# A one-core hybrid decoder block: TensorE's work put in written order, gates moved ahead of branch products, PSUM banks dealt out anew

## The chip, the cores and the metric

The kernel runs on one core of a Trainium2 chip. The metric is the device time of one execution in microseconds (us), lower is better. Three runs of the kernel before took 1508.08 us in the median (1503.97 to 1508.12). The profiled execution is a run of its own.

## What is computed

One decoder layer on 256 tokens of width 2048, in float32. The reference, cut to what matters:

```python
h = rmsnorm(x, norm_g)
proj = einsum('bsd,df->bsf', h, w_in)            # 2048 -> 18432 columns, 14 parts
ya = stick_breaking_attention(a_q, a_k, a_v) * silu(a_g)            # 8 heads of 128
yb = silu(layernorm(causal_depthwise_conv(b_a * sigmoid(b_b)))) * silu(b_g)   # width 31
yc = gelu(c_u) * spatial_mix(layernorm(gelu(c_v))) * silu(c_g)
yd = dilated_mixture(d_q, d_k, d_v) * silu(d_g)                     # 8 heads, 3 patterns
yproj = einsum('bsnc,ncd->bsnd', stack([ya, yb, yc, yd]), w_branch) # 4 x (1024 -> 2048)
gates = sigmoid(einsum('bsd,df->bsf', h, w_gate) + b_gate)          # 2048 -> 4 x 2048
x = x + einsum('bsd,de->bse', sum(gates * yproj), w_out)
out = rmsnorm(x, final_g)
```

## The kernel before

**Weights.** All weights stand in one array of blocks of 128x2048 floats, in the order in which they are used (`weight_plan`, L35). A block is fetched by one 1 MB DMA into one of three `st` buffers (L117). To keep float32 accuracy at the speed of a reduced format, each half block is split in two: ScalarE copies it rounded into `hi` (L130) and VectorE subtracts that from the original into `lo` (L131). There are five `hi` and five `lo` buffers of 128x1024; a half block's buffers come free when TensorE has used them, so up to two and a half blocks are ready ahead. The splits are put 300 instructions ahead in priority (L140).

**Two forms of product.** In the *feature form* (`mm_t`, L238) a block gives 128 features for all 256 tokens: 16 steps over the 2048 inputs, each a product of 512 columns (L245: hi weights by the activations' hi and lo parts side by side) and one of 256 columns (L248: lo weights by the hi part). `proj_t` (L272) makes two such features tiles in the two banks of one PSUM tile of `ps_mm`; `evac` (L264) then adds the two column halves, by ScalarE (L266) and VectorE (L267), for both features at once. A *pair* below is such a pair of blocks. In the *token form* (`mm_n`, L278) a block is the moving operand: 24 products of 512 columns (L286 to L288), for both halves of the tokens. Four blocks make 512 output columns over all 2048 inputs, two over a branch's 1024.

**Order of the stages.** d_v in the token form (with unnormalised x, while `make_h`, L213, computes the norm and writes the normalised activations' parts to `xhl`); b_a and b_b with their product `glu`; the 8 heads of d, each three pairs of q and k with their `scores`, `softmax`, `transpose` and `values` (L420 to L473); the layer norm of the convolution (L493); the gate stage of d; b_g and the gate stage of b; a_v, four head pairs of a (L532), the gate stage of a; c_v, the eight tiles of c, its gate stage; the output projection with the final norm.

**A gate stage** (`gate_proj`, L358) has four column blocks of 512. For each one: two bias products (L369) and 96 products into a `ps_mm` tile of two banks, ScalarE's sigmoid into `gt` (L375), then 48 products of the branch into the `ps_2` tile `psy`, which VectorE multiplies with the gate (L382, L384) and adds to `merged` (L385). In the last stage `sink` (L637) then transposes that block of `merged` (L642) and splits it into `mh` and `ml` for the output projection.

**What sets the order.** The program is written in one order; a scheduler that plays it through with estimated times then fixes each engine's instruction order: of the instructions whose inputs it expects to be ready it takes the one written first, priorities considered. That holds for all engines, TensorE too. The small products of the attention heads are written between the large ones by `later(n, fn)` and `tick` (L147 to L159): `fn` is written when n more ticks have passed. A pair has one tick, a gate block three. `flush` (L161) ends all that is pending at once; it stands ahead of each gate stage and behind the last. The 31 taps of the convolution for 8 channel blocks (L402 to L412, 248 VectorE instructions, mostly L412) are written nine at a time between the pairs of d, with a priority 100 lower; they only need `glu`, so they can be taken whenever VectorE has nothing older.

**PSUM** has 8 banks of 512 floats per partition: `ps_mm` two tiles of two banks (feature pairs, token blocks, gates, output, transposes of `sink`), `ps_2` one tile of two banks (branch products, attention's transposes and sums), `ps_s` two tiles of one bank (scores).

**The sums of an a pair** (L553): four products for the first of two heads into the first bank of `cc` (L557 to L560), VectorE's subtraction of it from `zm` (L561), then the same for the second head in the second bank.

Of the kernel before, what the change touches and what calls it, by code (L numbers as in the profile page):

```python
# [31 lines left out]
BRANCH = dict(a=0, b=1, c=2, d=3)  # L32


def weight_plan():  # L35

    plan = []

    def t(name, i):
        plan.append(("in", OFF[name] // P + i))  # L40

    def n(name):
        for c in range(2):
            for q in range(4):
                plan.append(("inN", OFF[name] // 512 + c, q))

    def gate(b):
        for c in range(4):
            for q in range(4):
                plan.append(("gateN", BRANCH[b] * 4 + c, q))  # L50
            for q in range(2):
                plan.append(("brN", BRANCH[b], c, q))
# [42 lines left out]
def hybrid_block(ctx: ExitStack, tc, w, x, xT, vec, bg, cst, dmask, sgu_wT, sgu_lg, sgu_lb, sgu_b, final_g, out):  # L95
# [117 lines left out]
    def make_h():  # L213
# [11 lines left out]
        T.matmul(pst[:, :S], ones, red[:, 0, :], start=True, stop=False)  # L225
        T.matmul(pst[:, :S], ones, red[:, 1, :], start=False, stop=True)
        rsqrt(rstd[:], pst[:, :S], float(D), [P, S])
        for q in range(4):
            for k in range(4 * q, 4 * q + 4):
                V.scalar_tensor_tensor(xt[:, k, :], xt[:, k, :], norm_g(k), rstd[:], op0=ALU.mult, op1=ALU.mult)  # L230
            ks = slice(4 * q, 4 * q + 4)
            split(xhl[:, ks, 0:S], xhl[:, ks, S:2 * S], xt[:, ks, :])
        for b in range(2):
# [4 lines left out]
    def mm_t(ps, j, weights, rhs, nk):  # L238

        for k in range(nk):  # L240
            hi, lo = weights[k // 8]
            o = (k % 8) * P

            def full(start, stop):
                T.matmul(ps[:, j, :], hi[:, o:o + P], rhs[:, k, :], start=start, stop=stop)  # L245

            def half():
                T.matmul(ps[:, j, 0:S], lo[:, o:o + P], rhs[:, k, 0:S], start=False, stop=False)  # L248

            if k < nk - 1:  # L250
# [6 lines left out]
    def unit_t(e0, e1):  # L257
        ps = ps_mm.tile([P, 2, 512], F32, tag="mm", name="ps")
        mm_t(ps, 0, next_weights(e0), xhl, KD)
        mm_t(ps, 1, next_weights(e1), xhl, KD)  # L260
        tick()
        return ps

    def evac(ps, dst):  # L264
        bt = ev_p.tile([P, 2, S], F32, tag="bt", name="bt")
        A.activation(bt[:], ps[:, :, S:2 * S], AF.Copy)  # L266
        V.tensor_add(dst, ps[:, :, 0:S], bt[:])  # L267
# [29 lines left out]
    def first_weights(q, expect):  # L297
# [17 lines left out]
        return res  # L315

    def proj_n(name, c, step=None, first=False):
        ps = ps_mm.tile([P, 2, 512], F32, tag="mm", name="psn")
        for q in range(4):
# [5 lines left out]
            if step is not None:  # L325
                step()
        if first and c == 0:
            make_h()
        return ps

    def proj_v(name, step=None, first=False):
        v = t8_p.tile([P, 2, BW], F32, tag="t8", name="v")
        for c in range(2):
            ps = proj_n(name, c, step=step, first=first)
            for tb in range(2):
# [21 lines left out]

    def gate_proj(b, y, first=False, sink=None, step=None):  # L358

# [4 lines left out]

        for c in range(4):
            g = bi * 4 + c
# [7 lines left out]
            gt = gt_p.tile([P, 2, 512], F32, tag="gt", name="gt")  # L374
            A.activation(gt[:], ps[:], AF.Sigmoid)  # L375
# [4 lines left out]
            m = merged[:, :, c * 512:(c + 1) * 512]  # L380
            if first:
                V.tensor_mul(m, psy[:], gt[:])  # L382
            else:
                V.tensor_mul(gt[:], psy[:], gt[:])  # L384
                V.tensor_add(m, m, gt[:])  # L385
            if sink is not None:
                later(1, lambda c=c: sink(c))
            if step is not None:
                step()

# [83 lines left out]

    for h0 in range(0, NH, 2):
        sg = proj_t(ft("d_g", h0), ft("d_g", h0 + 1))
        A.activation(sg[:], sg[:], AF.Silu)
        conv(9)
        d_head(h0, sg)
        d_head(h0 + 1, sg)  # L480


    def chan_sum(src):
        red = ev_p.tile([P, 2, S], F32, tag="bt", name="red")
        V.tensor_reduce(red[:, 0, :], src.rearrange("p c t -> p t c"), axis=AX.X, op=ALU.add)
        ps = ps_2.tile([P, 2, 512], F32, tag="a2", name="pcs")
        T.matmul(ps[:, 0, 0:S], ones, red[:, 0, :], start=True, stop=True)
        return ps[:, 0, :]

    def bc8(ap):  # L490
        return ap.unsqueeze(1).to_broadcast([P, KB, S])

    def conv_norm():  # L493
        pm = chan_sum(cv[:])
        mean = sm_p.tile([P, S], F32, tag="mean", bufs=1, name="mean")
# [3 lines left out]
        A.activation(csq[:], cv[:], AF.Square)  # L499
        pv = chan_sum(csq[:])  # L500
        rsqrt(mean[:], pv[:, 0:S], float(BW), [P, S])
        V.tensor_mul(cv[:], cv[:], bc8(mean[:]))
# [4 lines left out]
    conv_norm()  # L507
    flush()
    gate_bias()
# [6 lines left out]
    for i in range(0, 8, 2):  # L516
        bg = proj_t(ft("b_g", i), ft("b_g", i + 1))
        A.activation(bg[:], bg[:], AF.Silu)
        V.tensor_mul(bg[:], bg[:], cv[:, i:i + 2, :])
        put_y(yb, i, 2, bg[:])  # L520

    flush()
    gate_proj("b", yb)


# [6 lines left out]
    def a_pair(h0):  # L532
        sg = proj_t(ft("a_g", h0), ft("a_g", h0 + 1))
        A.activation(sg[:], sg[:], AF.Silu)
        zm = sc_p.tile([P, 2, 384], F32, tag="e1", bufs=1, name="zm")
# [45 lines left out]

    flush()
    gate_proj("a", ya)


# [39 lines left out]
    for i in range(8):  # L625
        ug = proj_t(ft("c_u", i), ft("c_g", i))
        A.activation(ug[:, 0, :], ug[:, 0, :], AF.Gelu_apprx_tanh)
        A.activation(ug[:, 1, :], ug[:, 1, :], AF.Silu)
        later(2, lambda i=i, ug=ug: c_mix(i, ug))

    flush()

# [4 lines left out]
    def sink(c):  # L637
        pt = ps_mm.tile([P, 4, S], F32, tag="mm", name="pt")
        for f in range(4):
            for tb in range(2):  # L640
                o = c * 512 + f * P
                T.transpose(pt[:, f, tb * P:(tb + 1) * P], merged[:, tb, o:o + P], ident)  # L642
        ks = slice(4 * (c % 2), 4 * (c % 2) + 4)
        A.activation(mh[c // 2][:, ks, :], pt[:], AF.Copy)
        V.tensor_sub(ml[c // 2][:, ks, :], pt[:], mh[c // 2][:, ks, :].bitcast(F32))

    gate_proj("c", yc, sink=sink)
    flush()

# [47 lines left out]
    for tb in range(2):  # L697
        ps = ps_mm.tile([P, 2, 512], F32, tag="mm", name="pso")
        for q in range(4):
# [65 lines left out]
```

## Time and profile before

| what | us |
|---|---|
| median of three runs | 1508.08 |
| the profiled execution's own time | 1508.27 |
| its span in the profile | 1506.6 |
| TensorE busy (98%) | 1479.1 |
| VectorE busy (63%) | 944.4 |
| ScalarE busy (50%) | 760.2 |
| weights read by DMA at 185 GB/s over the span | 277.18 MB |

PE is TensorE's products, PEld its weight loads, DVE is VectorE, ACT is ScalarE, SP and POOL issue DMAs. Products are pipelined: a product of 512 columns is shown as 0.39 us long but the next begins 0.23 us after it, so a busy TensorE is read from the starts and from the idle time in brackets, not from the lengths. "DVE lo L131" is the instruction of line 131 that writes the tile `lo`. The views used below are the page's overview, the list of waits, the table of time windows, the timeline of one engine in a window, and the answer for one source line.

### The profile page before, as it was taken

The page shows a single profiled execution, that of the slowest core. Times are in us where ns is not written, and L with a number is a line of the kernel's source. Part 1 is how long each engine was busy: PE and PEld are TensorE (multiplying, and loading weights), DVE is VectorE, ACT ScalarE, POOL GpSimd, SP SyncE. Part 2 cuts the span into 40 slices and gives each one's busy share as a digit, 9 for nine tenths or more (in the row PEclk, how much of TensorE's full clock was granted, in tenths as well). Part 3 has the DMA queues.
Part 4 walks back from the last instruction along what each step waited for, and adds up shares of the span by engine and source line. Part 5 has one row for each costly group of instructions (what it writes and reads, how often), then busy time and mean ns, then how long its engine had stood idle before and what let it go on. Part 6 is the DMA issues. An engine that isn't in the chain of part 4 may idle for free.

```text
span 1506.6 us, 18648 instructions
## 1 busy us (share of the span) xinstructions
PE 1479.1 (98%) x7484; PEld 1255.4 (83%) x7484; DVE 944.4 (63%) x1249; ACT 760.2 (50%) x860; POOL 10.2 (1%) x22
## 2 busy tenths in 40 slices
PE   7999999999999999999999999999999999999997
PEld 5888888888888788888888888887888888888786
DVE  8899999866566754555545455554545666555454
ACT  7644445564454644454444466654444667444352
POOL 0000000000000000000000000000000000000000
PEclk9999999999999999999999999999999999999999
DMA  8555554445444555555555545444555555555562
GB/s 302 211 195 184 180 187 177 169 166 191 173 168 170 201 203 186 192 195 189 186 186 195 194 168 172 168 177 154 196 195 195 181 183 198 200 190 177 192 217 84
DMA packets 41318, 280.47 MB, mean 186 GB/s; under 512 B 4784, under 2 KB 4784, under 8 KB 8592
## 3 DMA queue, kind: packets, MB, share of 16 engines
q1 hardware_dynamic: 38880, 272.00, 50.5%
q0 software_dynamic: 1632, 6.24, 1.3%
q8 instruction: 58, 0.95, 0.3%
q10 hardware_dynamic: 720, 1.06, 0.2%
q14 instruction: 28, 0.23, 0.0%
HBM read 277.18 MB, written 2.10 MB: 185 GB/s over the span
## 4 chain that ended last, share of the span: by engine, by line
PE 97%; ACT 1%; DVE 1%; DMA 1%; issue 0%; DVEq 0%; ACTq 0%
PE ps L245 30%; PE ps L248 15%; PE psg L286 8%; PE psg L288 8%; PE psg L287 8%; PE psy L286 4%; PE psy L288 4%; PE psy L287 4%; PE psn L287 3%; PE psn L288 3%; PE psn L286 3%; PE pso L286 2%; PE pso L287 2%; PE pso L288 2%; DMA xt<-in_xT_dram 0%; PE psg L369 0%
## 5 line engine op out<-in xcount | busy, mean ns | idle before, releaser
L131 DVE TENSOR_TENSOR lo<-st,hi 128x1024 fp32r<-128x1024 f32 (+1 forms) x506 | 616.0, 1219 | 460.7 <-ACT hi L130 459.2
L130 ACT ACTIVATE hi<-st 128x1024 fp32r<-128x1024 f32 (+1 forms) x506 | 533.4, 1056 | 671.7 <-PE ps L245 262.3
L245 PE MATMUL ps<-xhl,hi 128*128 128x512 f32 x1920 | 675.5, 398 | 0.0
L248 PE MATMUL ps<-xhl,lo 128*128 128x256 f32 x1920 | 519.5, 281 | 0.0
L245 PEld LDWEIGHTS ps<-xhl,hi 128*128 128x128 f32 x1920 | 355.2, 188 | 74.6
L248 PEld LDWEIGHTS ps<-xhl,lo 128*128 128x128 f32 x1920 | 362.3, 189 | 9.6
L286 PE MATMUL psg<-hi,xhl 128*128 128x512 f32 x512 | 201.0, 393 | 1.1 <-ACT hi L130 1.1
L288 PE MATMUL psg<-hi,xhl 128*128 128x512 f32 x512 | 200.3, 391 | 0.0
L287 PE MATMUL psg<-lo,xhl 128*128 128x512 f32 x512 | 200.2, 391 | 0.0
L286 PEld LDWEIGHTS psg<-hi,xhl 128*128 128x128 f32 x512 | 96.4, 188 | 21.6 <-ACT hi L130 1.7
L288 PEld LDWEIGHTS psg<-hi,xhl 128*128 128x128 f32 x512 | 96.6, 189 | 20.2
L287 PEld LDWEIGHTS psg<-lo,xhl 128*128 128x128 f32 x512 | 96.6, 189 | 20.0
L412 DVE SCALAR_TENSOR_TENSOR cv<-glu,vec_sb,cv 128x255 f32<-128x255 f32 (+26 forms) x240 | 100.8, 463 | 0.2
L286 PE MATMUL psy<-hi,y 128*128 128x512 f32 x256 | 99.6, 389 | 0.0
L287 PE MATMUL psy<-lo,y 128*128 128x512 f32 x256 | 99.6, 389 | 0.0
L288 PE MATMUL psy<-hi,y 128*128 128x512 f32 x256 | 99.6, 389 | 0.0
L288 PEld LDWEIGHTS psy<-hi,y 128*128 128x128 f32 x256 | 48.1, 188 | 10.0
L287 PEld LDWEIGHTS psy<-lo,y 128*128 128x128 f32 x256 | 48.1, 188 | 10.0
L286 PEld LDWEIGHTS psy<-hi,y 128*128 128x128 f32 x256 | 48.1, 188 | 9.9
L286 PE MATMUL psn<-hi,xhl 128*128 128x512 f32 x128 | 49.8, 389 | 0.0
L287 PE MATMUL psn<-lo,xhl 128*128 128x512 f32 x128 | 49.8, 389 | 0.0
L288 PE MATMUL psn<-hi,xhl 128*128 128x512 f32 x128 | 49.8, 389 | 0.0
(207 smaller groups left out, 1105.2 us busy)
## 6 DMA issues: line engine op xcount, KB each, us to landing
st<-in_w_dram SPq DMA_DIRECT2D x254, 1024.0 KB, 4.8
xr<-in_x_dram POOLq DMA_DIRECT2D x8, 256.0 KB, 3.9
xt<-in_xT_dram SPq DMA_DIRECT2D x3, 512.0 KB, 8.7
st<-in_w_dram SPq DMA_DIRECT2D x4, 256.0 KB, 5.3
st<-in_w_dram SPq DMA_DIRECT2D x2, 512.0 KB, 7.4
fg<-in_final_g_dram POOLq DMA_DIRECT2D x1, 1024.0 KB, 6.8
out_dram<-r SPq DMA_DIRECT2D x4, 256.0 KB, 3.2
out_dram<-r ACTq DMA_DIRECT2D x4, 256.0 KB, 3.5
```

The costliest lines, as they stand in the source:

```text
L130: A.activation(hi, src, AF.Copy)
L131: V.tensor_sub(lo, src, hi.bitcast(F32))
L245: T.matmul(ps[:, j, :], hi[:, o:o + P], rhs[:, k, :], start=start, stop=stop)
L248: T.matmul(ps[:, j, 0:S], lo[:, o:o + P], rhs[:, k, 0:S], start=False, stop=False)
L286: T.matmul(ps[:, tb, :], lh(k0 + kk, 0, tb), hi[:, o:o + 512], start=st, stop=False)
L287: T.matmul(ps[:, tb, :], lh(k0 + kk, 0, tb), lo[:, o:o + 512], start=False, stop=False)
L288: T.matmul(ps[:, tb, :], lh(k0 + kk, 1, tb), hi[:, o:o + 512], start=False, stop=sp)
L412: V.scalar_tensor_tensor(dst, src, wc, dst, op0=ALU.mult, op1=ALU.add)
```

## The change

- **TensorE in written order.** `tc.manual_schedule(engines={PE})`: TensorE's instructions run in the order in which the program writes them; the other engines are still ordered by the scheduler.
- **Gate stage.** The four gate blocks g0 to g3, branch products y0 to y3 and sinks s0 to s2 are written as g0 g1 y0 g2 s0 y1 g3 s1 y2 y3 s2; the plan of weights follows. Sink 3 stands in the output projection's first block, ahead of its last quarter.
- **PSUM.** `ps_mm` has one tile of two banks; two tiles of one bank (`ps_t`) take the feature tiles, each evacuated by itself, and `sink`'s transposes in two halves. The token blocks and output blocks alternate between `ps_mm` and `ps_2`. `make_h`'s and the channel sums' products move to `ps_s`.
- **`make_h`** is written in three pieces: its squares and sums behind d_v's first block, its sum products and what follows behind the first quarter of the second block, the products for `rstd_n` behind the third quarter. d_v's blocks are both evacuated after both are written.
- **The convolution's norm** is written in three pieces from d's head 6 on, one and three pairs ahead of the gate stage; the remaining taps are written there.
- **The flushes are gone**: what is pending at the end of a stage is written at the ticks of the gate stage that follows.

The diff, cut to its core:

```diff
+GATE_ORDER = [(e[0], int(e[1])) for e in "g0 g1 y0 g2 s0 y1 g3 s1 y2 y3 s2".split()]
...
-    ps_mm = ctx.enter_context(tc.tile_pool(name="psm", bufs=2, space=bass.MemoryType.PSUM))
+    ps_t = ctx.enter_context(tc.tile_pool(name="pst", bufs=2, space=bass.MemoryType.PSUM))
+    ps_mm = ctx.enter_context(tc.tile_pool(name="psm", bufs=1, space=bass.MemoryType.PSUM))
     ps_2 = ctx.enter_context(tc.tile_pool(name="ps2", bufs=1, space=bass.MemoryType.PSUM))
     ps_s = ctx.enter_context(tc.tile_pool(name="pss", bufs=2, space=bass.MemoryType.PSUM))
+
+    ctx.enter_context(tc.manual_schedule(engines={mybir.EngineType.PE}))
...
         V.tensor_add(red[:], red[:], rd2[:])
-        pp = ps_2.tile([P, 2, 512], F32, tag="a2", name="pp")
-        pst, psn = pp[:, 0, :], pp[:, 1, :]
+        yield
+        pst = ps_s.tile([P, 512], F32, tag="s", name="pst")
         T.matmul(pst[:, :S], ones, red[:, 0, :], start=True, stop=False)
...
-    def proj_t(e0, e1):
-        ps = unit_t(e0, e1)
+    def proj_t(e0, e1, funcs=(None, None)):
+
         dst = qk_p.tile([P, 2, S], F32, tag="qk", name="dst")
-        evac(ps, dst[:])
+        for j, e in enumerate((e0, e1)):
+            ps = ps_t.tile([P, 512], F32, tag="t", name="ps")
+            mm_t(ps, next_weights(e), xhl)
+            bt = ev_p.tile([P, S], F32, tag="bt", name="bt")
+            A.activation(bt[:], ps[:, S:2 * S], AF.Copy)
+            V.tensor_add(dst[:, j, :], ps[:, 0:S], bt[:])
+            if funcs[j] is not None:
+                A.activation(dst[:, j, :], dst[:, j, :], funcs[j])
+        tick()
         return dst
...
     def proj_n(name, c, step=None, first=False):
-        ps = ps_mm.tile([P, 2, 512], F32, tag="mm", name="psn")
+        ps = (ps_2.tile([P, 2, 512], F32, tag="a2", name="psn") if c else
+              ps_mm.tile([P, 2, 512], F32, tag="mm", name="psn"))
...
+            if first and c and q in (0, 2):
+                next(parts[0])
         if first and c == 0:
-            make_h()
+            parts.append(make_h())
+            next(parts[0])
...
+        gts = {}
+
+        def gate(c):
             g = bi * 4 + c
             ps = ps_mm.tile([P, 2, 512], F32, tag="mm", name="psg")
...
+            gts[c] = gt_p.tile([P, 2, 512], F32, tag="gt", name="gt")
+            A.activation(gts[c][:], ps[:], AF.Sigmoid)
+
+        def branch(c):
             psy = ps_2.tile([P, 2, 512], F32, tag="a2", name="psy")
             for q in range(2):
                 mm_n(psy, next_weights(("brN", bi, c, q)), 4 * q, y_lh, q == 0, q == 1)
             tick()
...
+        for s, c in GATE_ORDER:
+            if s != "s":
+                (gate if s == "g" else branch)(c)
+            elif sink is not None:
+                sink(c)
...
+        if h0 == 6:
+            conv(len(taps))
+            conv_norm()
+        d_head(h0 + 1, sg)
...
-    flush()
     gate_proj("a", ya)
...
     def sink(c):
-        pt = ps_mm.tile([P, 4, S], F32, tag="mm", name="pt")
-        for f in range(4):
...
+        for f0 in (0, 2):
+            pt = ps_t.tile([P, 2, S], F32, tag="t", name="pt")
+            for f in range(2):
...
     for c in range(3):
-        ps = ps_mm.tile([P, 2, 512], F32, tag="mm", name="pso")
+        ps = (ps_2 if c % 2 else ps_mm).tile([P, 2, 512], F32, tag="a2" if c % 2 else "mm", name="pso")
         for q in range(4):
+            if c == 0 and q == 3:
+                sink(3)
             mm_n(ps, next_weights(("out", c, q)), 4 * q, m_lh, q == 0, q == 3)
```

More of the change, by code (lines that the diff above doesn't have):

```diff
@@ L47, in gate @@
     def gate(b):
[L48 to L52, printed above, removed]
+        for s, c in GATE_ORDER:
+            if s == "g":
+                for q in range(4):
+                    plan.append(("gateN", BRANCH[b] * 4 + c, q))
+            elif s == "y":
+                for q in range(2):
+                    plan.append(("brN", BRANCH[b], c, q))
     n("d_v")
@@ L232, in make_h @@
             split(xhl[:, ks, 0:S], xhl[:, ks, S:2 * S], xt[:, ks, :])
+        yield
+        psn = ps_s.tile([P, 512], F32, tag="s", name="psn")
         for b in range(2):
@@ L235, in make_h, with mm_t @@
         V.tensor_copy(rstd_n[:], psn[:, 0:2])
-    def mm_t(ps, j, weights, rhs, nk):
-        for k in range(nk):
+        yield
+    def mm_t(ps, weights, rhs):
+        for k in range(KD):
             hi, lo = weights[k // 8]
@@ L332, in proj_v @@
         v = t8_p.tile([P, 2, BW], F32, tag="t8", name="v")
-        for c in range(2):
-            ps = proj_n(name, c, step=step, first=first)
+        pss = [proj_n(name, c, step=step, first=first) for c in range(2)]
+        for c, ps in enumerate(pss):
             for tb in range(2):
@@ L356, in gate_bias, with gate_proj @@
         V.tensor_sub(bgr[32:64, :], b[32:64, :], bgr[32:64, :].bitcast(F32))
-    def gate_proj(b, y, first=False, sink=None, step=None):
+    def gate_proj(b, y, first=False, sink=None):
         bi = BRANCH[b]
@@ L363, in y_lh @@
             return y[:, k, part * S + tb * P:part * S + (tb + 1) * P]
-        for c in range(4):
+        gts = {}
+        def gate(c):
             g = bi * 4 + c
@@ L379, in gate_proj @@
             tick()
-            m = merged[:, :, c * 512:(c + 1) * 512]
+            m, gt = merged[:, :, c * 512:(c + 1) * 512], gts.pop(c)
             if first:
@@ L385, in gate_proj @@
                 V.tensor_add(m, m, gt[:])
[L386 to L389, printed above, removed]
+        for s, c in GATE_ORDER:
+            if s != "s":
+                (gate if s == "g" else branch)(c)
+            elif sink is not None:
+                sink(c)
     vd = proj_v("d_v", first=True)
@@ L473, in d_head, with chan_red, chan_sum, conv_norm2 @@
             later(1, lambda g=g, qk=qk, qs=qs: scores(g, qk, qs))
[L475 to L488, printed above, removed]
     def bc8(ap):
         return ap.unsqueeze(1).to_broadcast([P, KB, S])
+    def chan_red(src):
+        red = ev_p.tile([P, S], F32, tag="bt", name="red")
+        V.tensor_reduce(red[:], src.rearrange("p c t -> p t c"), axis=AX.X, op=ALU.add)
+        return red
+    def chan_sum(red):
+        ps = ps_s.tile([P, 512], F32, tag="s", name="pcs")
+        T.matmul(ps[:, 0:S], ones, red[:], start=True, stop=True)
+        return ps
     def conv_norm():
-        pm = chan_sum(cv[:])
+        red = chan_red(cv[:])
+        later(1, lambda: conv_norm2(red))
+    def conv_norm2(red):
+        pm = chan_sum(red)
         mean = sm_p.tile([P, S], F32, tag="mean", bufs=1, name="mean")
@@ L499, in conv_norm, with conv_norm3 @@
         A.activation(csq[:], cv[:], AF.Square)
-        pv = chan_sum(csq[:])
-        rsqrt(mean[:], pv[:, 0:S], float(BW), [P, S])
-        V.tensor_mul(cv[:], cv[:], bc8(mean[:]))
+        red = chan_red(csq[:])
+        later(2, lambda: conv_norm3(red))
+    def conv_norm3(red):
+        pv = chan_sum(red)
+        rs = sm_p.tile([P, S], F32, tag="mean", bufs=1, name="rs")
+        rsqrt(rs[:], pv[:, 0:S], float(BW), [P, S])
+        V.tensor_mul(cv[:], cv[:], bc8(rs[:]))
         for i in range(8):
@@ L505, in conv_norm @@
                          scale=vec_sb[:, V_LG + i:V_LG + i + 1])
-    conv_norm()
-    flush()
+    for h0 in range(0, NH, 2):
+        sg = proj_t(ft("d_g", h0), ft("d_g", h0 + 1), (AF.Silu, AF.Silu))
+        conv(9)
+        d_head(h0, sg)
+        if h0 == 6:
+            conv(len(taps))
+            conv_norm()
+        d_head(h0 + 1, sg)
     gate_bias()
@@ L580, in hybrid_block @@
         a_pair(h0)
-    flush()
     gate_proj("a", ya)
@@ L637, in sink @@
     def sink(c):
-        pt = ps_mm.tile([P, 4, S], F32, tag="mm", name="pt")
-        for f in range(4):
[L640 to L645, printed above, removed]
+        for f0 in (0, 2):
+            pt = ps_t.tile([P, 2, S], F32, tag="t", name="pt")
+            for f in range(2):
+                for tb in range(2):
+                    o = c * 512 + (f0 + f) * P
+                    T.transpose(pt[:, f, tb * P:(tb + 1) * P], merged[:, tb, o:o + P], ident)
+            ks = slice(4 * (c % 2) + f0, 4 * (c % 2) + f0 + 2)
+            A.activation(mh[c // 2][:, ks, :], pt[:], AF.Copy)
+            V.tensor_sub(ml[c // 2][:, ks, :], pt[:], mh[c // 2][:, ks, :].bitcast(F32))
     gate_proj("c", yc, sink=sink)
-    flush()
     fg = y_p.tile([P, D], F32, tag="y", name="fg")
@@ L697, in hybrid_block @@
     for tb in range(2):
-        ps = ps_mm.tile([P, 2, 512], F32, tag="mm", name="pso")
+        ps = (ps_mm if tb else ps_2).tile([P, 2, 512], F32, tag="mm" if tb else "a2", name="pso")
         for q in range(4):
```

31 lines of the change are left out of this document (7 added, 24 removed).

## The prediction, made before the change was run

> **What bounds the kernel now.** I read the page's overview first, then the waits of TensorE, then the busy time in short windows around those waits, then the timelines of single engines at the places that the change touches.
>
> ```profile
> PE 1479.1 (98%) x7484; PEld 1255.4 (83%) x7484; DVE 944.4 (63%) x1249; ACT 760.2 (50%) x860; POOL 10.2 (1%) x22
> ```
>
> TensorE is busy for 1479.1 of 1506.6 us. The number of products does not change, so the change can win only from the 27.5 us in which TensorE stands idle, and from the time in which it runs slowly after standing idle. Who makes it wait:
>
> ```profile
> PE psn L286 <- ACT xuh L209: 5.9, 1, 5.9
> PE pt L642 <- DVE merged L385: 3.7, 1, 3.7
> PE psg L369 <- ACT gt L375: 3.7, 2, 1.8
> ```
>
> The first is the wait for the first weights and x; the change does not touch it. The other two are the places that the new order is about: the entry to the gate stages of d and a, where the attention's tail is flushed, and the end of the last gate stage. The windows around them (columns: PE, PEld, DVE, ACT, POOL busy, then the granted clock):
>
> ```profile
> 507.40:510.80 3.40, 1.44 (x5) 0.99 (x6) 3.30 (x7) 3.06 (x5) 0.00 (x0) 1.00 0.54 183
> 510.80:514.20 3.40, 3.40 (x10) 2.62 (x9) 1.96 (x1) 0.00 (x0) 0.00 (x0) 0.50 0.35 147
> 514.20:524.00 9.80, 9.31 (x42) 7.59 (x42) 3.62 (x5) 8.82 (x13) 2.26 (x3) 1.00 0.62 214
> 1016.00:1019.40 3.40, 1.56 (x7) 1.05 (x6) 1.22 (x2) 3.36 (x4) 0.00 (x0) 0.99 0.64 270
> 1019.40:1022.80 3.40, 3.02 (x11) 2.30 (x9) 0.00 (x0) 0.69 (x1) 0.00 (x0) 0.50 0.00 0
> 1401.70:1405.10 3.40, 1.28 (x6) 0.74 (x4) 3.00 (x3) 1.06 (x1) 0.53 (x1) 1.00 0.39 106
> 1405.10:1411.90 6.80, 5.24 (x17) 4.50 (x18) 2.64 (x3) 1.02 (x1) 0.00 (x0) 0.50 0.62 258
> 19.30:22.70 3.40, 1.82 (x9) 1.16 (x7) 3.40 (x4) 3.40 (x8) 0.54 (x1) 1.00 0.99 410
> ```
>
> The reader sees two costs at each place. First the idle time itself. Second, the stretch behind a window in which TensorE was busy for 1.44, 1.56 or 1.28 of 3.40 us (38 to 46%) is granted half the clock for 3.4 us. At 19.3, with 1.82 of 3.40 (54%), the clock stayed whole. So idle time of 1.9 us or more in one such window is paid about once and a half.
>
> **The change part by part. What it removes.** Entry to d's gates: 3.40 - 1.44 = 1.96 idle, 3.40 / 2 = 1.70 for the half clock, 9.80 - 9.31 = 0.49 behind it: 4.15 us. Entry to a's gates: 1.84 idle, then 0.38 idle and 3.02 / 2 = 1.51 at half clock: 3.73 us. The end: 2.12 and 1.56 idle, 5.24 / 2 = 2.62 at half clock: 6.30 us. Sum **-14.2 us**: the tails of the heads now stand behind 10 us and more of gate products, and s3 behind three quarters of an output block. This is the most that the change can win; the three places are the whole of what TensorE loses after its start.
>
> **What it adds: g0 to g1.** `ps_mm` has one tile now, and g1 follows g0. So g1's first bias product waits until ScalarE's sigmoid has read g0, and in written order nothing else can go ahead of it. How long that takes stands in the b stage of the trace before, where it was hidden by y0 and the second tile:
>
> ```profile
> 690.24 1.06 ACT L130 ACTIVATE hi<-st 128x1024 fp32r<-128x1024 f32 x1 [1.66 <-PE psg L288]
> 691.32 1.28 ACT L375 ACT_TABLE_LOAD   x1
> 692.61 1.03 ACT L375 ACTIVATE gt<-psg 128x1024 f32<-128x1024 f32 x1
> ```
> ```profile
> 689.81 0.39 PE L288 MATMUL psg<-hi,xhl 128*128 128x512 f32 x1
> 690.04 0.39 PE L286 MATMUL psy<-hi,y 128*128 128x512 f32 x1
> ```
>
> The last gate product frees a `hi` buffer at the moment in which it makes the gate ready, and the split has the higher priority: 1.06 us of split, 1.28 us of table load (the stage before used another function), 1.03 us of sigmoid, done at 693.64. The next product would have begun at 690.04, and with some 0.05 us for the signal it begins at 693.69: 3.65 us. Each of the four stages has one such place, 14.6 us. Some small products stand in the gap (three transposes in d, the last sums in a, four products in c); I take 1.0 off: **+13.6 us**. The bounds are 4 x 1.2 = 4.8 (sigmoid first, table loaded ahead) and 14.6. A gap of 3.65 us leaves one 3.4 us window with at least half of it, 1.83 us, idle, which is between the windows that were throttled and the one that was not; I count the half clock for three of four, 3 x 1.70 = **+5.1 us** (0 to 6.8).
>
> For the clock the trace shows throttling after windows that were 38 to 46% busy. [...]
>
> **y2 to y3.** `psy` is a single tile as before, and y3 follows y2 directly. The end of the last stage shows what it waits for:
>
> ```profile
> 1402.60 0.39 PE L288 MATMUL psy<-hi,y 128*128 128x512 f32 x1
> 1406.66 1.94 PE L642 MATMUL pt<-cst_sb,merged 128*128 128x128 f32 x8 [3.68 <-DVE merged L385]
> ```
> ```profile
> 1403.02 1.23 DVE L384 TENSOR_TENSOR gt<-psy,gt 128x1024 f32<-128x1024 f32 x1 [0.40 <-PE psy L288]
> ```
>
> VectorE's multiplication ends at 1404.25, the next product could begin at 1404.30 instead of 1402.83: 1.47 us, four times, **+5.9 us**. 1.47 of 3.40 us leaves the window 57% busy, so no half clock. The wait has no other product behind it on TensorE that could fill it. The pairs g1 y0 g2, y1 g3 y2 are spaced by 11 us and more of products on other tiles and cost nothing.
>
> **s3 in the output block.** Its eight transposes stand right ahead of the quarter that reads them, through ScalarE's copy and VectorE's subtraction. With half the tile per copy I estimate 1 us: ScalarE's split of 1.06 us and half of a 1.03 us pass over 1024 columns (the two L130 and L375 rows above), less the transposes ahead of it, eight in 1.94 us at half clock: **+1.0 us** (0 to 2).
>
> **The start.** The norm's sum products move from inside d_v's first block to behind the second block's first quarter.
>
> ```profile
> 31.43 0.59 PE L225 MATMUL pp<-red,cst_sb 128*128 128x256 f32 x2
> ...
> 57.12 0.39 PE L288 MATMUL psn<-hi,xul 128*128 128x512 f32 x1
> 57.34 0.39 PE L245 MATMUL ps<-xhl,hi 128*128 128x512 f32 x1
> 57.57 0.28 PE L248 MATMUL ps<-xhl,lo 128*128 128x256 f32 x1
> 57.69 0.40 PE L245 MATMUL ps<-xhl,hi 128*128 128x512 f32 x1
> ```
> ```profile
> 55.98 1.22 DVE L131 TENSOR_TENSOR xhl<-xt,xhl 128x1024 fp32r<-128x1024 f32 x1
> ```
>
> The second block's 96 products, one each 0.227 us, end at 57.34, so its first quarter ends about 57.34 - 72 x 0.227 = 41, less the products for the sums and `rstd_n`, some 1 us: 40. The chain that ended with the last quarter of `xhl` at 57.20 thus begins 8.5 us later and would end at 65.7 if it were as long. TensorE needs that quarter after 12 of 16 steps of the first feature tile, at 57.34 + 12 x 0.35 = 61.5 (a step is the 0.35 us from 57.34 to 57.69). So up to 4.2 us of waiting; nothing if VectorE, which stands free for those 8.5 us, gets weight splits done ahead. I take **+1.5 us**.
>
> **Feature tiles.** A bank must be emptied while the other is filled, within one block.
>
> ```profile
> 217.06 0.38 PE L427 MATMUL s<-dst 128*128 128x128 f32 x2
> ```
> ```profile
> 219.58 0.69 DVE L267 TENSOR_TENSOR dst<-ps,bt 128x512 f32<-128x512 f32 x1
> ```
>
> Even where VectorE is fullest, a pair that ended at 217.2 was emptied at 220.27, in 3.1 us with both features; a block lasts 16 x 0.35 = 5.6 us. What covers it is the other bank's block; 0.
>
> **The heads of d.** This is the part that I know least. The first head's weights were late by the written order, and TensorE went on with other blocks:
>
> ```profile
> 205.20 0.38 PE L427 MATMUL s<-dst 128*128 128x128 f32 x2
> ```
> ```profile
> 244.31 0.54 DVE L448 TENSOR_SCALAR e<-e,sm 128x128 f32<-128x128 f32 x2
> ```
> ```profile
> 252.25 0.27 PE L455 MATMUL po<-cst_sb,e 128*128 128x128 f32 x1
> ```
> ```profile
> L412 DVE SCALAR_TENSOR_TENSOR cv<-glu,vec_sb,cv 128x255 f32<-128x255 f32 (+26 forms) x240 | 100.8, 463 | 0.2
> ```
>
> The last scores of head 0 begin at 205.20; one pair later, at 217.06, the transposes are due in written order; the softmax was done at 244.85 because VectorE runs convolution taps between its steps (240 taps, 100.8 us), and they ran at 252.25. Had VectorE kept its order, TensorE would stand for 27.8 us less the weight splits that a standing TensorE doesn't ask for, about half: 14 us. The scheduler will plan VectorE around the waiting TensorE, and taps done in the wait are not done later. Bounds 0 and 25 (a second head); I take **+5 us**, nearer to the lower end, since the taps run out soon.
>
> **The sums of a.**
>
> ```profile
> 940.23 0.40 PE L560 MATMUL cc<-spl,one_r 128*128 128x384 f32 x1
> ...
> 945.52 0.34 PE L557 MATMUL cc<-sph,one_r 128*128 128x384 f32 x1
> ```
> ```profile
> 941.38 0.55 DVE L561 TENSOR_TENSOR zm<-zm,cc 128x384 f32<-128x384 f32 x1
> ```
>
> The second head's sums read tiles that are ready, and yet came 5.3 us after the first's: I read that as a wait for VectorE's subtraction of the first. In written order TensorE stands from about 940.6 to 941.93 for it. Three pairs at 1.0 to 1.4 us (the fourth lies in the g0 gap): **+3.0 us** (0 to 5).
>
> **The sum.** -14.2 + 13.6 + 5.1 + 5.9 + 1.0 + 1.5 + 0 + 5.0 + 3.0 = +20.9 us on the profiled execution's 1508.27: **1529 us**. That execution lies 0.2 us above the median of the runs, so nothing is to be corrected.
>
> **The rivals.** *Faster: the gaps at the gates close.* If ScalarE takes the sigmoid ahead of the split with its table loaded, the g0 gap is 1.2 us and throttles nothing: 4.8 + 5.9 + 1.0 - 14.2 = -2.5, 1506; if the scheduler, which sees TensorE wait, also finds cover for y3, it goes toward 1508.3 - 14.2 = 1494. It decides at a g0 gap below about 1.3 us. Against it stands that the split went first in the trace, with higher priority and the same release. I give 0.14 to a time under 1503.5.
> *No change:* the waits added are about those removed, or the change does little of what it says, since TensorE's order, taken from the same written program, was close to the written one already outside the places named: 0.12.
> *Slower by more: the convolution.* TensorE's waits in the d heads at their upper bound of 25 us, with half clock behind them, and the start at 4.2: 1529 + 20 + 3 = 1552. For it speaks the row of VectorE's 244.31; against, that taps end once done. 0.12.
> My forecast, the gate gaps with part of the small waits, 1513 to 1545, has the remaining 0.62.
>
> **How the numbers follow.** What two kernels' runs can tell apart here is about 0.3%, 4.5 us. Slower by more than that: forecast and the third rival, 0.74; within it 0.12; faster 0.14. The range takes the no-change case whole and most of the convolution case: 1504 to 1550.
>
> **What would show it.** Right: TensorE's waits list "psg L369 <- ACT gt L375" four times or so at about 3.5 us, and "psy L286 <- DVE" (L382 or L384) four times at about 1.3; half-clock windows behind the first; no wait at `pt L642`; idle at L455 between 215 and 250. TensorE's idle time rises from 27.5 to 40 us or more. Wrong: g1's bias products begin within 1.3 us of g0's last product, or TensorE's idle time falls below 20 us.

## The result, and the profile after

The changed kernel took 1555.06 us in the median of four runs (1550.04 to 1555.65), against 1506.65 us before (1503.97 to 1508.12): the ratio is 1.0316, 95% interval 1.0288 to 1.0344. It is slower, as forecast, but by 48 us and not by 21, and outside the stated range. The profiled execution took 1555.39 us.

From the page of the changed kernel, TensorE's line:

```profile
PE 1495.8 (96%) x7484; PEld 1265.5 (81%) x7484; DVE 949.8 (61%) x1313; ACT 772.7 (50%) x941; POOL 10.2 (1%) x22
```

The span is 1553.7 us. TensorE stands idle for 1553.7 - 1495.8 = 57.9 us (27.5 before), 30.4 more; and the same 7484 products keep it busy for 16.7 us more (1479.1 before). Together they make up the 47.1 us between the spans. Who makes it wait, from its list of waits (total, times, longest; the lines are those of the changed kernel: L389 is the sigmoid, L473 the transposes of d's heads, L584 the sums of a):

```profile
PE po L473 <- DVE e L466: 14.1, 2, 11.3
PE psg L383 <- ACT gt L389: 11.2, 4, 3.5
PE cc L584 <- DVE zm L588: 6.5, 4, 2.0
PE psn L292 <- ACT xuh L216: 5.8, 1, 5.8
PE psy L292 <- DVE gt L400: 4.2, 3, 1.4
PE psn L293 <- DVE lo L138: 2.2, 2, 1.6
PE psy L292 <- DVE merged L398: 1.4, 1, 1.4
PE s L448 <- DVE e L138: 0.8, 1, 0.8
PE pso L292 <- ACT mh L667: 0.8, 1, 0.8
PE ps L255 <- DVE xhl L138: 0.7, 2, 0.4
PE pso L294 <- DVE ml L668: 0.6, 1, 0.6
```

The transposes' wait at the end, on which the change was to win, is gone. The wait for a sigmoid, which stood at the entries to the gates of d and a (3.7 us in two), is not: before, the third gate block's bias product waited there for g0's sigmoid, and now g1's does, in all four stages (11.2 us). New are the first, the third, the two of `psy`, and small ones at the scores and at sink 3 (`pso`).

The lengths of the stages, each from the start of its first product with weights (the gates' bias products left aside) to that of the next stage's first (worked out from TensorE's timelines):

| stage | before, us | after, us | difference |
|---|---|---|---|
| d_v, then b_a and b_b | 141.9 | 142.9 | +1.0 |
| heads of d | 335.0 | 356.4 | +21.4 |
| gate stages of d, b, a, c | 552.3 | 565.2 | +12.9 |
| heads of a | 147.4 | 158.5 | +11.1 |
| output and end | 98.3 | 99.4 | +1.1 |
| the rest (b_g, a_v, c_v, c) | 225.8 | 225.3 | -0.4 |

*The heads of d.* The timeline of TensorE at the first head's transposes, and VectorE's at the end of that wait:

```profile
219.59 0.39 PE L255 MATMUL ps<-xhl,hi 128*128 128x512 f32 x1
231.32 0.45 PE L473 MATMUL po<-cst_sb,e 128*128 128x128 f32 x1 [11.34 <-DVE e L466]
```
```profile
226.03 0.27 DVE L464 TENSOR_TENSOR e<-e 128x128 f32<-128x128 f32 x1
226.24 0.15 DVE L462 RECIPROCAL sm<-sm 128x2 f32<-128x2 f32 x1
226.31 0.39 DVE L464 TENSOR_TENSOR e<-e 128x256 f32<-128x256 f32 x1
226.63 1.95 DVE L430 SCALAR_TENSOR_TENSOR cv<-glu,vec_sb,cv 128x232 f32<-128x232 f32 x5
228.50 0.61 DVE L465 TENSOR_TENSOR e<-e 128x128 f32<-128x128 f32 x2
229.04 1.94 DVE L430 SCALAR_TENSOR_TENSOR cv<-glu,vec_sb,cv 128x231 f32<-128x231 f32 x5
230.91 0.53 DVE L466 TENSOR_SCALAR e<-e,sm 128x128 f32<-128x128 f32 x2
```

TensorE stands still while VectorE runs five taps of the convolution (L430) between each two of the last steps of the softmax it waits for (L464, L465, L466). These ten taps are 3.9 of the 11.3 us. The first 6 us of the wait lie ahead of the rows shown: VectorE does two weight splits, two evacuations and seven more taps there, and ScalarE a split, an evacuation, a table load of 1.28 us and the exponentials.

*The sums of a.* The same two engines in the second head pair's sums:

```profile
933.10 0.39 PE L587 MATMUL cc<-spl,one_r 128*128 128x384 f32 x1
935.46 0.44 PE L584 MATMUL cc<-sph,one_r 128*128 128x384 f32 x1 [1.97 <-DVE zm L588]
```
```profile
932.26 1.22 DVE L138 TENSOR_TENSOR lo<-st,hi 128x1024 fp32r<-128x1024 f32 x1
933.39 0.42 DVE L278 TENSOR_TENSOR dst<-ps,bt 128x256 f32<-128x256 f32 x1
933.73 1.22 DVE L138 TENSOR_TENSOR lo<-st,hi 128x1024 fp32r<-128x1024 f32 x1
934.86 0.55 DVE L588 TENSOR_TENSOR zm<-zm,cc 128x384 f32<-128x384 f32 x1
```

The subtraction (L588) is 0.55 us, but an evacuation and a weight split stand ahead of it in VectorE's order.

*The clock.* Windows of the changed kernel, columns as before (busy times, then PE's granted clock):

```profile
219.50:231.20 11.70, 0.48 (x4) 0.16 (x2) 11.70 (x30) 4.24 (x7) 0.00 (x0) 0.66 0.36 144
231.20:237.00 5.80, 5.68 (x21) 5.04 (x22) 5.80 (x19) 1.12 (x2) 0.00 (x0) 0.50 0.01 3
...
933.00:936.70 3.70, 1.73 (x11) 1.41 (x10) 3.70 (x6) 2.80 (x4) 0.00 (x0) 1.00 0.82 283
936.70:940.10 3.40, 3.40 (x12) 2.88 (x11) 0.64 (x2) 0.84 (x1) 0.00 (x0) 0.50 0.64 270
```

Behind the long wait TensorE works for 5.8 us at half clock (0.50). Behind a wait of 1.97 us, in a window in which it was busy for 1.73 of 3.70 us (47%; 1.44 of the last 3.41 us, 42%), it works for 3.4 us at half clock. The trace of the changed kernel has half-clock stretches of 3.41, 6.83 and 13.65 us ahead of the last product; 3.41 us of it are called a half-clock window below. Filled with work such a window is counted at 1.7 us, half of its length; this is an estimate from the granted 0.50 (in the one from 718.24 us on products of 512 columns begin 0.43 us apart, from 721.71 us on 0.23). Most of the 16.7 us of longer busy time come from this: behind the start TensorE was busy for 38.1 us at half clock, before for 11.7, and half of the difference is 13.2 us. The other 3.5 us are not accounted for. (The mean granted clock, 0.983 against 0.994, would give 17.4 us, but it also counts half-clock time in which TensorE stood idle.)

### The profile page after: what moved, and what is told of

It is laid out like the page before. It is cut to its first block, busy times and chain, and to the rows that moved or that the text cites. A ratio compares the mean times of both kernels' runs of the same rounds, so it can differ in the third digit from the quotient of the medians.

```text
span 1553.7 us, 18803 instructions
## 1 busy us (share of the span) xinstructions
PE 1495.8 (96%) x7484; PEld 1265.5 (81%) x7484; DVE 949.8 (61%) x1313; ACT 772.7 (50%) x941; POOL 10.2 (1%) x22
## 4 chain that ended last, share of the span: by engine, by line
PE 84%; DVE 8%; ACT 4%; issue 2%; DMA 1%; DVEq 0%; ACTq 0%
PE ps L255 24%; PE ps L258 12%; PE psg L292 8%; PE psg L293 8%; PE psg L294 8%; PE psy L292 4%; PE psy L294 4%; PE psy L293 4%; DVE lo L138 3%; DVE cv L430 3%; PE pso L294 2%; PE psn L292 2%; PE psn L294 2%; PE psn L293 2%; PE pso L292 2%
## 5 line engine op out<-in xcount | busy, mean ns | idle before, releaser
L255 PEld LDWEIGHTS ps<-xhl,hi 128*128 128x128 f32 x1920 | 359.1, 190 | 78.5 <-DVE xhl L138 1.3
L258 PEld LDWEIGHTS ps<-xhl,lo 128*128 128x128 f32 x1920 | 366.0, 191 | 9.5
L292 PEld LDWEIGHTS psg<-hi,xhl 128*128 128x128 f32 x512 | 98.3, 192 | 20.9
L430 DVE SCALAR_TENSOR_TENSOR cv<-glu,vec_sb,cv 128x252 f32<-128x252 f32 (+26 forms) x240 | 99.6, 457 | 0.2
L278 DVE TENSOR_TENSOR dst<-ps,bt 128x256 f32<-128x256 f32 x120 | 49.9, 416 | 0.1
L292 PE MATMUL psn<-hi,xhl 128*128 128x512 f32 x128 | 49.8, 389 | 0.0
```

Of the source, the lines that this page charges most:

```text
L255: T.matmul(ps[:], hi[:, o:o + P], rhs[:, k, :], start=start, stop=stop)
L258: T.matmul(ps[:, 0:S], lo[:, o:o + P], rhs[:, k, 0:S], start=False, stop=False)
L278: V.tensor_add(dst[:, j, :], ps[:, 0:S], bt[:])
L292: T.matmul(ps[:, tb, :], lh(k0 + kk, 0, tb), hi[:, o:o + 512], start=st, stop=False)
L430: V.scalar_tensor_tensor(dst, src, wc, dst, op0=ALU.mult, op1=ALU.add)
```

## The experiments

**Theory:** TensorE in written order now pays for VectorE's and ScalarE's delay in four places (heads of d, sums of a, g0 to g1, y2 to y3), and each wait is paid again in part by the half clock behind it. **Rivals:** the new deal of PSUM, with two evacuations where there was one, slows the feature stages whatever the order; VectorE is simply too full, so that TensorE must wait for it somewhere; the half clock costs little. Where a kernel was executed once, its time says little below some 5 us, the spread of the kernel before and of the changed one from run to run; its waits and half-clock windows in the profile say more. Span, busy and idle time in the table are those of the profiled execution.

| run | time, us | executions | span | TensorE busy | idle |
|---|---|---|---|---|---|
| before, profiled | 1508.27 | 1 | 1506.6 | 1479.1 | 27.5 |
| changed, profiled | 1555.39 | 1 | 1553.7 | 1495.8 | 57.9 |
| e1 changed, order by the scheduler | 1521.29 | 2 | 1519.0 | 1482.6 | 36.4 |
| e2 before, written order | 1570.96 | 2 | 1569.6 | 1490.9 | 78.7 |
| e3 sums ahead of subtractions | 1542.85 | 1 | 1541.1 | 1488.8 | 52.3 |
| e4 few taps | 1534.98 | 1 | 1533.3 | 1487.2 | 46.1 |
| e5 transposes one pair later | 1545.72 | 1 | 1544.0 | 1492.9 | 51.1 |
| e6 g1 in spare banks | 1530.87 | 1 | 1529.2 | 1482.2 | 47.0 |
| e7 y3 in another tile | 1546.55 | 1 | 1544.8 | 1489.4 | 55.4 |
| e8 g0's gap filled | 1545.33 | 1 | 1543.6 | 1496.1 | 47.5 |
| e9 all mended | 1501.92 | 7 | 1498.4 | 1475.5 | 22.9 |
| e10 all mended, order by the scheduler | 1495.15 | 5 | 1493.4 | 1473.4 | 20.0 |
| e11 norm behind the heads | 1545.70 | 1 | 1544.0 | 1489.3 | 54.7 |

### e1 and e2: the order and the rest, apart

e1, in the changed kernel:
```diff
-    ctx.enter_context(tc.manual_schedule(engines={mybir.EngineType.PE}))
```


> The changed kernel, but TensorE's order is left to the scheduler again; PSUM, gate order and everything else as changed. Theory (written order exposes VectorE's latency in the heads of d and in the sums of a): the waits at the transposes and at the second head's sums are gone, 21 us and 11 us of stage time, and the scheduler fills part of the gate gaps: 1510 to 1523 us. Rival (the new PSUM deal, one bank per feature tile with twice as many evacuations, makes the feature stages slower whatever the order): stays within 10 us of 1555.

Measured: 1521.29 us, ratio to before 1.0097 (1.0068 to 1.0126). The heads of d take 331.8 us (335.0 before), b_a and b_b 90.7 (90.5 before). Its waits:

```profile
PE psg L382 <- ACT gt L388: 10.0, 4, 3.5
PE psn L291 <- ACT xuh L215: 6.0, 1, 6.0
PE ps L254 <- DVE dst L277: 2.8, 6, 1.0
```

The rival that blames the feature tiles falls: the single banks cost 2.8 us of waits, and these two stages are as long as before. The waits for transposes and sums are down to 2.0 us in all. The wait from g0 to g1 stays, 10.0 us: it belongs to the single `ps_mm` tile, and the scheduler put nothing in it. So the rest of the change does cost time without written order, at the gates: e1 is still 14.5 us slower than the kernel before. Written order makes up the other 34 us of the loss.

e2, in the kernel before, ahead of the weight plan:
```diff
+    ctx.enter_context(tc.manual_schedule(engines={mybir.EngineType.PE}))
```


> The kernel before with one line more: TensorE in written order. Theory: the heads of d and the sums of a wait as in the changed kernel (+21, +11 us), and the old program's flushes and its norm at the start, which the change had moved, now stand open too (about 10 us at each of d's and a's gates, 8 at the start): 1560 to 1575 us, slower than the changed kernel. Rival (PSUM deal is the cause): within 10 us of 1507.

Measured: 1570.96 us, ratio 1.0427 (1.0396 to 1.0457). From its waits:

```profile
PE po L457 <- DVE e L450: 20.3, 2, 11.7
PE pcs L489 <- DVE red L487: 9.4, 1, 9.4
PE pp L236 <- DVE rstd L192: 8.0, 1, 8.0
PE cc L559 <- ACT sph L132: 6.4, 1, 6.4
```

Written order alone costs 64 us. What the change rearranged for it (norms in pieces, no flushes, gates ahead) removes the last three of these and, with the waits that it adds at the gates counted in, wins back 16 us; it leaves the heads of d.

### e3: the sums of a

```diff
                 T.matmul(c[:, 0:384], tri_r, spl[:, j, :], start=False, stop=True)
-                V.tensor_sub(zm[:, j, :], zm[:, j, :], c[:, 0:384])
+            for j in range(2):
+                V.tensor_sub(zm[:, j, :], zm[:, j, :], cc[:, j, 0:384])
```


> The changed kernel with both heads' sums of an a pair written ahead of the two subtractions. Theory (the second head's products wait for the first's subtraction): three waits of 1.6 to 2.0 us and the half clock behind each go, the a stage is 11 us shorter: about 1544 us. Rival (the products would wait for the split spl anyway): the wait moves to the first sums, under 3 us gained: 1552 or more.

Measured: 1542.85 us. The wait at the sums is gone from the list, the heads of a take 147.6 us instead of 158.5 (147.4 before). The theory's 11 us are there: three waits of 2.0 us and three half-clock windows (0.50 from 936.69, 977.65 and 1018.61 us on in the changed kernel), counted at 1.7 us each.

### e4, e5 and e11: the heads of d

e4 leaves out the 240 taps behind each channel block's first, so branch b is another function:
```diff
+            if lag:
+                continue
             t = V_CW + i * TAPS + TAPS - 1 - lag
```


> The changed kernel with the 240 taps of the convolution behind the first of each channel left out (8 of 248 remain, so branch b is another function). Theory (VectorE runs taps between the steps of the first heads' softmax): the 11.3 us wait at the transposes in d is gone with its half clock, d's feature stage is 15 to 18 us shorter, 1537 to 1541 us; the 2.9 us wait later in the stage, behind the convolution's norm, stays. Rival (the softmax chain is too long for one pair by itself, with its table load): the wait stays above 5 us and comes at every head, within 5 us of 1555.

Measured: 1534.98 us, 2 us below the range expected; the heads of d take 340.6 us instead of 356.4, as expected. Its waits from 150 to 489 us, all through the heads of d:

```profile
PE po L475 <- DVE e L468: 2.8, 1, 2.8
```

The 11.3 us are gone, no other head's transposes are late except head 6's. The softmax does fit into one pair; the taps make it late. That it is their place, and not only the load that they put on VectorE, this run can't tell; e5 bears on it.

e5, in the changed kernel:
```diff
-            later(1, transpose)
+            later(2 if h < 6 else 1, transpose)
```


> The changed kernel with the transposes of heads 0 to 5 of d written one pair later. Theory (the order is wrong for VectorE's delay, the work itself is no longer): the 11.3 us wait and its half clock are gone, d's feature stage is 13 to 16 us shorter, 1539 to 1542 us; the 2.9 us wait of head 6 stays. Rival (VectorE's queue is simply full there, so TensorE must wait for it somewhere): another wait of 5 us or more appears at the scores or the feature tiles, less than 6 us gained: 1549 or more.

Measured: 1545.72 us, the heads of d 346.7 us, 9.7 less and not 13 to 16. Waits from 150 to 495 us:

```profile
PE po L473 <- DVE e L466: 5.6, 2, 2.9
PE ps L255 <- DVE dst L278: 0.8, 2, 0.7
PE s L448 <- DVE e L138: 0.7, 1, 0.7
```

The expectation was too high: of the 11.3 us 2.9 stay, at head 0's transposes a pair later: VectorE's timeline there has ten taps, three weight splits, a split of q and k and an evacuation between the softmax's steps (226 to 235 us). The other 2.8 us are head 6's. No other wait of weight came up, so the rival, VectorE full in any order, holds for about a quarter of it at most.

e11, in the changed kernel:
```diff
-        if h0 == 6:
-            conv(len(taps))
-            conv_norm()
         d_head(h0 + 1, sg)
+    conv(len(taps))
+    conv_norm()
```


> The changed kernel with the convolution's norm written behind the last head of d instead of behind head 6. Theory (its two long VectorE operations, 2.28 and 3.94 us, stand inside head 6's softmax): the 2.9 us wait for head 6's transposes is gone and with it one half-clock window, d's feature stage 4 us shorter; head 7's transposes, in the gate stage, may be late instead, which the wait for g0's sigmoid hides: 1549 to 1552 us. Rival (head 6 is late for another reason): the wait stays, 1555.

Measured: 1545.70 us, 9.4 less, where 3 to 6 were expected. The 2.8 us wait is gone from the heads of d (350.6 us long, 5.9 less). A wait of 2.5 us comes up at head 7's transposes in the gate stage, and the wait for g0's sigmoid there falls to 0.4 us, as it lies behind the same gap. The norm's long VectorE operations (2.28 and 3.94 us at 476.87 and 481.14 us in the changed kernel) did cause head 6's wait. The idle time fell by 3.2 us only; the rest is 6.5 us less busy time. Of that 1.7 us is the half-clock window behind head 6's wait, as expected; the others, a net three windows fewer at the gates and the sums of a, fell otherwise.

### e6, e7 and e8: the gates and the clock

e6 gives g1 the two feature banks (the core of the edit; the sigmoid of g1 then reads them one by one):
```diff
+            if c == 1:
+                pair = [ps_t.tile([P, 512], F32, tag="t", name="psg") for _ in range(2)]
+            else:
+                both = ps_mm.tile([P, 2, 512], F32, tag="mm", name="psg")
+                pair = [both[:, tb, :] for tb in range(2)]
```


> The changed kernel with g1 of each gate stage in the two one-bank feature tiles, which stand free there, so that it needn't wait for g0's sigmoid. Theory: the four waits at the gates' bias products go (11.2 us) with the half clock behind them (8 us): 1535 to 1538 us. Rival (something else, the attention's tail, stands behind the same place): the waits move to the sums and transposes in the gates, less than 10 us gained: 1545 or more.

Measured: 1530.87 us, 24.2 less. No wait at the gates' bias products is left in its list, idle time fell by 10.9 us and busy time by 13.6 us. This is more than the 17 to 20 us expected. The gate stages are 21.0 us shorter: the waits, and six half-clock windows that stood behind them (two each in d and c, one each in b and a: in the changed kernel the clock is 0.50 over 530.51:537.33, 1336.05:1342.88, 718.24:721.65 and 1059.57:1062.99). The heads of a are 3.0 us shorter although their waits at the sums are the same: two of their three half-clock windows didn't come. What such a gap is made of, in the changed kernel's b stage:

```profile
714.52 1.06 ACT L137 ACTIVATE hi<-st 128x1024 fp32r<-128x1024 f32 x1 [1.66 <-PE psg L294]
715.59 1.28 ACT L389 ACT_TABLE_LOAD   x1
716.88 1.02 ACT L389 ACTIVATE gt<-psg 128x1024 f32<-128x1024 f32 x1
```
```profile
714.09 0.39 PE L294 MATMUL psg<-hi,xhl 128*128 128x512 f32 x1
717.96 0.99 PE L383 MATMUL psg<-bgr,sel 128*128 128x512 f32 x2 [3.48 <-ACT gt L389]
```

Split, table load, sigmoid, and the bias product 3.87 us behind the last gate product, 3.64 more than the usual 0.23: the row of the prediction, almost to the digit. The other three places have 3.92, 3.88 and 3.92 us from product to product.

e7:
```diff
-            psy = ps_2.tile([P, 2, 512], F32, tag="a2", name="psy")
+            psy = (ps_mm if c == 3 else ps_2).tile([P, 2, 512], F32, tag="mm" if c == 3 else "a2", name="psy")
```
with the output blocks' tiles swapped.


> The changed kernel with y3 in the gates' tile, which is free by then, and the output blocks' tiles swapped. Theory: four waits of 1.4 us go, no half clock is involved: 1549 us, 5.6 us less. Rival: the wait moves to the next stage's first product, 1554 or more.

Measured: 1546.55 us. Its waits have no `psy` left, but this one:

```profile
PE psn L292 <- DVE gt L400: 2.8, 2, 1.4
```

Half the wait moved, as the rival says, to a_v and c_v, whose first block uses the same tile. Idle time fell by 2.5 us. That the time fell by 8.5 us, more than either side expected, is 6.4 us of busy time: 5.1 of them are three half-clock windows fewer, at the gates of b, a and c, behind waits for the sigmoid that are as long as in the changed kernel. The expectation's 5.6 us for this wait can't be told from that in one execution.

e8 adds 14 products that nobody reads behind g0, into a feature bank:
```diff
+            if (s, c) == ("g", 0):
+                spare = ps_t.tile([P, 512], F32, tag="t", name="spare")
+                for n in range(14):
+                    T.matmul(spare[:], xhl[:, n, 0:P], xhl[:, n, :], start=True, stop=True)
```


> The changed kernel with 14 extra products of 512 columns into a spare bank, read by nobody, behind g0 in each gate stage: 14 x 0.227 = 3.2 us of the wait of 3.3 to 3.7 us are filled with useless work, and g1 begins when it did. Theory (a wait is paid about once and a half, through the half clock behind it): the wait costs what it did, the half-clock windows behind the four gates are gone, 8 us less: about 1547 us. Rival (the clock falls for another reason, or costs nothing): 1555, or more by what the products overhang.

Measured: 1545.33 us, 9.7 less, with 56 more products. Windows from d's g0 on and from b's g0 on:

```profile
527.00:531.00 4.00, 4.00 (x18) 2.99 (x17) 1.65 (x2) 3.49 (x5) 0.00 (x0) 1.00 1.00 395
531.00:537.00 6.00, 6.00 (x28) 4.95 (x27) 1.23 (x1) 1.92 (x2) 0.00 (x0) 1.00 0.16 52
712.00:718.30 6.30, 5.98 (x27) 4.61 (x26) 0.65 (x1) 2.71 (x3) 0.00 (x0) 1.00 0.34 142
718.30:721.70 3.40, 3.40 (x17) 2.82 (x16) 1.80 (x2) 1.13 (x2) 0.00 (x0) 1.00 0.29 53
```

The clock stays whole (1.00) where it was halved in the changed kernel (0.50): none of the six half-clock windows of the gates is left. The gaps in d, b and c are as long as they were (3.93, 3.88 and 3.93 us from product to product), filled with useless work; in a, where the wait was shorter, the filling overhangs and the gap is 1.6 us longer. The gate stages are 7.2 us shorter all the same: the half clock behind these waits was a cost of its own, and with the idle time filled it did not come. The rest of the 9.7 us is half-clock windows elsewhere that fell otherwise.

### e9 and e10: all of it mended

e9 puts together e3, e5 (heads 0 to 6), e6, e7 with the token blocks' tiles swapped too, and sink 3 a quarter earlier (the only piece not shown above); e10 is e9 with TensorE's order left to the scheduler.
```diff
-            if c == 0 and q == 3:
+            if c == 0 and q == 2:
                 sink(3)
```


> The changed kernel with all waits mended that the runs found: both heads' sums ahead of the subtractions, transposes of heads 0 to 6 one pair later, g1 in the two feature banks, y3 in the gates' tile with the token blocks and output blocks dealt out to fit, sink 3 one quarter earlier. Theory (the waits and their half clock are the whole of the loss, and the change's removal of the two gate entries and the end is real): 48 us less 3 to 8 us left in the heads of d and 1 us at the start, and the 14 us of the prediction gained against before only as far as those allow: 1496 to 1502 us, faster than before by 5 to 10 us. Rival (written order has a price of its own, or the waits mended come back elsewhere): 1507 or more.

> The same with TensorE's order left to the scheduler. Theory (what pays is the placing of the work, and written order gives nothing that the scheduler wouldn't give with the same program): within 5 us of the mended kernel in written order, without the waits left in d. Rival (written order keeps TensorE from choosing badly at the gates): 8 us or more slower than it, with waits at the gates' bias products.

Measured: e9 1501.92 us, ratio to before 0.9970 (0.9959 to 0.9982); e10 1495.15 us, ratio 0.9926 (0.9913 to 0.9938). Both are faster than both kernels, than the one before by 0.3% and 0.7%: little, but the intervals exclude 1. e9's waits and e10's, each without the first 5.9 and 5.8 us for x:

```profile
PE po L482 <- DVE e L475: 2.9, 1, 2.9
PE psn L294 <- DVE lo L138: 2.1, 2, 1.6
PE ps L255 <- DVE dst L278: 1.2, 2, 0.8
PE s L457 <- DVE e L138: 0.7, 1, 0.7
PE ps L255 <- DVE xhl L138: 0.5, 2, 0.3
```
```profile
PE psn L293 <- DVE lo L137: 3.0, 3, 1.6
PE ps L254 <- DVE dst L277: 1.8, 3, 1.0
```

The waits found account for the whole of the loss: with them mended the changed kernel is 53 us faster, no half-clock window is left ahead of the last product, and the gate stages take 537.3 us, 15.0 less than before. The heads of d are still 7.2 us longer than before; e9's longest wait, head 0's softmax, is there, and e10 hasn't it. The theory for e10 allowed 5 us between the two; e10 is 6.8 us faster, so neither side of the expectation holds to the number, but the rival falls: written order gave nothing here that the scheduler didn't give from the same program, and kept a wait that the scheduler fills.

## Why the prediction was wrong

**Right, step by step.** g0 to g1: 3.64 us in the b stage against 3.65 worked out, and the other three gaps are within 0.05 us of it; the idle time in them is 11.2 us against 13.6. y2 to y3: 5.6 us of waits (4.2 and 1.4) against 5.9. Sink 3: 1.4 (0.8 and 0.6) against 1.0. The start, with b_a and b_b: 1.0 against 1.5. Feature tiles: 0.2 us of waits against 0. The removal can't be seen apart in the changed kernel, since a wait for g0's sigmoid stands at the gates of d and a again; e9, whose gate stages have no wait and no half clock, has them 15.0 us shorter than before, against 14.2 worked out. Together the gate stages and the output came out at +14.0 us; the sum for them was -14.2 + 13.6 + 5.1 + 5.9 + 1.0 = 11.4. That it came so near is luck in part: the half clock behind g0 was six windows, 10.2 us against the 5.1 counted, and the idle time made up for half of that.

**Wrong: the heads of d.** The step that failed is "I take +5 us, nearer to the lower end, since the taps run out soon". It measured +21.4. The working had 14 us from VectorE's order of before and 25 as an upper end, and the reason to go below both, that the scheduler plans VectorE around a waiting TensorE, was the opposite of what happened: from 225 us on the wait leaves VectorE without weight splits, and taps fill it, five between each two of the softmax's last steps (the timeline above; e4, without them, has no such wait). Of the 21.4 us, 15 are idle (14.1 in two waits, 0.8 at the scores); the half clock is 2.8 us behind the long wait (5.68 / 2) and 1.7 behind the second; some 2 us are in neither and stay open. That the norm's own move put the second wait, 2.8 us at head 6, there (e11) wasn't foreseen at all.

**Wrong: the sums of a.** "Three pairs at 1.0 to 1.4 us (the fourth lies in the g0 gap): +3.0 us (0 to 5)" measured +11.1. The wait was read rightly, its size not: VectorE's subtraction doesn't come next but behind an evacuation and a split, so a wait is 2.0 us; and behind each of the three waits stands a half-clock window (0.50, the 3.41 us ahead of it busy for 1.44), three times 1.7 us, which the step left out although the prediction had read such windows itself.

**The rivals.** The third, the convolution in the way at its upper bounds (1552 us, 0.12), came nearest in time, and the heads of d did cost 21.4 of its 25; but its 4.2 us for the start were 1.0, and the sums of a, which it left at 3, filled the place: its time was right in part by luck. The sum of the first rival, -2.5, leaves out the 9.5 us that the forecast has for the start, d and a; with them it is +7.0, 1515 us.

So the direction and most of the mechanisms stood in the text. Two terms sized too low, both without the half clock behind their waits, make up some 24 of the 26 us missed.

## What to carry to other kernels

TensorE in written order waited here for the slowest delay behind each written distance (11.3 us at d's first transposes), so each distance is to be checked against the time at which the producer really finished in the trace before, with the filler that its engine runs between the steps counted in. A wait on TensorE is to be priced with the clock behind it, everywhere and not only at the largest, and as a range: here a wait of 2 us cost nothing more (two of three in e6) or 1.7 us more (all three in the changed kernel), one of 3.1 to 3.5 us from nothing (e7, b) to 3 us more (the changed kernel, d and c). A second PSUM tile for back-to-back blocks was worth 24 us in the changed kernel (e6), the scheduler's order 34 (e1); with the tiles and the distances mended the order was worth 7 (e9 against e10). Look for the free bank and for the distances first; what is left for the order is then small.

## What the runs showed of the hardware

In the changed kernel a single wait of 1.97 us at the sums of a was followed by 3.41 us at half clock (0.50 over 936.69:940.11), the 3.41 us ahead busy for 1.44 (42%); the four waits of 1.4 us for y3's tile had none of their own. In e8 a wait of 1.61 us at the start was followed by one, in a window busy for 1.80 of 3.41 us (53%). But a wait did not always bring it: of the same three waits at the sums of a, all three were followed by a half-clock window in the changed kernel, two in e4, e8 and e11, one in e6; and in e7 the clock stayed whole behind the 3.48 us wait at b's gates (711.56 to 715.04 us), which in the changed kernel had one. In e7 the idle time fell into two windows of 3.41 us, each busy for about half (1.63 and 1.71 us); in the changed kernel one window had only 0.28 us of work. So the prediction's limit, between 46 and 54% busy, is not a sharp one in these runs: 48 and 50% kept the clock in e7, 53% did not in e8. Which windows were hit thus depended on where the wait fell, and a small edit ahead of it changed the time by several us: e7 and e11 lost 6.4 and 6.5 us of busy time with the same products. Filling the gaps at the gates with products that nobody reads kept the clock whole (1.00) and made the run 9.7 us shorter (e8).
